# Modulation vectors from four stationary columns, and the first projections multiplied part by part

## The chip, the cores and the metric

One core of a Trainium2 chip runs the whole program. The metric is device time in microseconds (us) for one execution. The engines are called as in the profile: PE (TensorE, matmul), PEld (its weight loads), DVE (VectorE), ACT (ScalarE), POOL (GpSimd), SP (SyncE, which issues most DMAs).

## The reference, cut to what matters

The model is a block on 1024 tokens of width 1024 with a context of 256 tokens (an adaptive norm, a gated linear recurrence in two directions, a Fourier branch, 16 experts), and then a second mixer block. The change lies in its first steps only:

```
mx = silu(c)     @ w_ada + b_ada      # shift, scale, ... for the tokens
mc = silu(c_ctx) @ w_ada + b_ada      # the same for the context
pc = (rmsnorm(ctx, g) * (1 + csc1) + csh1) @ w_in    # gates, k, v of the context
px = (rmsnorm(x, g)   * (1 + sc1)  + sh1)  @ w_in    # all projections of the tokens
qk = silu(conv(px[q, k]));  gates -> log-sigmoid, running sums and maxima (scans)
```

Of `w_ada` only the first 2048 of 6144 columns (shift and scale of the first norm) are used in these steps.

## The kernel before, in words

Every large product is computed as three products of 32-bit operands that are split in a high and a low part: ACT copies the high part, DVE subtracts it from the operand to get the low part, and `mm3` (line 359) multiplies high by high, high by low and low by high into one PSUM bank. For a weight block of 128 x 1024, ACT and DVE each run one instruction for this (`_split`, line 234).

Each engine runs its instructions in the order in which the program emits them. All are issued through the wrapper at line 67, so that every row of the profile has the line L67; rows are told apart by their tiles: `w` split weights, `raw` weights as loaded, `silr` the split of silu(c), `ctx` and `x` the inputs, `hc` the modulated context (high and low), `hT` the modulated tokens, `tm` the modulated value before its split, `gt` the gate arrays, `qk` and `ko` convolution outputs, `pm` and `pa` the two groups of four PSUM banks, `wg` the gate weights.

The start (`start`, line 433) has these stages:

1. SP issues the eight 1 MB row blocks of `w_ada`, then the context (1 MB), the first gate weights come on ACT's queue; the tokens (4 MB) and two blocks of `w_in` follow after the first block of `w_ada` is used.
2. For each of the eight blocks: split in halves of 1024 columns, then `mm3` with a stationary operand of two columns (c and c_ctx), 12 matmuls of 512 columns in each block, 96 in all, into four banks.
3. Sums of squares and norm of the context, 16 transposes of it into four `pa` banks, copies of the two rows of results, 16 small transposes of them, and six small DVE instructions that form shift and scale.
4. Modulation of the context, in eight pieces k of 128 channels: ACT writes the high part, DVE the value, then DVE or POOL (in turn) subtracts for the low part.

Then `ctx_pass` (line 787) multiplies gates and values of the context, and `px_front` (line 866) the projections of the tokens, beginning with blocks 4 to 7 of 128 columns (the k half), each for tokens 0 to 511, tokens 512 to 1023, and the context. `tok` and `chan` call `pump`, which between matmul groups emits steps of work that waits in lanes: lane 0 holds `prep` (transposes and modulation of the tokens) and then the convolutions, lane 1 the gate work and the context's convolutions. A planner with its own cost model (`Plan`) decides by `until` and `calm` when a step is emitted; it is only a model, and the chip then runs what was emitted. The first token block is multiplied in the order tokens 0 to 511, context, tokens 512 to 1023, while `prep` goes on.

Of the kernel before, what the change touches and what calls it, by code (L numbers as in the profile page):

```python
# [9 lines left out]
FT = mybir.dt.float32  # L10
# [142 lines left out]
class Kern:  # L153
# [228 lines left out]
    def consts(self):  # L382
# [12 lines left out]
        self.silr = c([2, 16], "silr", FR)  # L395
        self.sx = c([8], "sx")
        self.shx = c([8], "shx")
# [5 lines left out]
        self.sctx, self.shctx, self.dnc = (self.state.t[:, i:i + 8] for i in (1976, 1984, 1992))  # L403
# [28 lines left out]

    def start(self):
# [7 lines left out]
        self.raw_max, self.limit, self.ahead, self.sub_max = 8, 8, 0, 0  # L441
        self.prefetch()
        nc.sync.dma_start(cs.t[:, :2048].rearrange("p (a d) -> p a d", a=2),
                          I["ctx"].rearrange("(a p) d -> p a d", p=128))
        xs = [self.slot(FT, "x") for _ in range(4)]
        xv = [xs[t // 2].t[:, (t % 2) * 1024:(t % 2) * 1024 + 1024] for t in range(8)]

        def load_x(p):
            nc.sync.dma_start(xs[p].t[:, :2048].rearrange("p (a d) -> p a d", a=2),
                              I["x"][p * 256:(p + 1) * 256].rearrange("(a p) d -> p a d", p=128))  # L450
        st = self.stat
        tm = self.slot(FT, "tm")

        def sumsq(tiles, a, both=False):
            for t, v in enumerate(tiles):
                o = st[:, a + t:a + t + 1]
                if both and t % 2:
                    nc.vector.scalar_tensor_tensor(self.hT[7].t[:, 0:1024], v, 1.0, v, op0=OP.mult, op1=OP.mult, accum_out=o)
                else:
                    nc.scalar.activation(tm.t[:, 0:1024], v, AF.Square, accum_out=o)  # L460

        def norm(tiles, a, engs=(nc.vector,)):
            n = len(tiles)
            self.inv_sqrt(st[:, 16 + a:16 + a + n], st[:, a:a + n], 1.0 / D, EPS)
            for t, v in enumerate(tiles):
                f = st[:, 16 + a + t:17 + a + t]
                e = engs[t % len(engs)]
                if e is nc.scalar:
                    e.activation(v, v, AF.Copy, scale=f)
                else:  # L470
                    e.tensor_scalar(v, v, f, None, op0=OP.mult)

        def modulate(items):
            for ps, hi, lo, tmp, s, sh, eng in items:
                nc.scalar.activation(hi, ps, AF.Identity, scale=s, bias=sh)
            for ps, hi, lo, tmp, s, sh, eng in items:
                nc.vector.tensor_scalar(tmp, ps, s, sh, op0=OP.mult, op1=OP.add)
            for ps, hi, lo, tmp, s, sh, eng in items:
                eng.tensor_sub(lo, tmp, hi.bitcast(FT))

        self.wg = self.load_wg()
        nc.scalar.dma_start(self.wr, I["w_r"])


        nc.scalar.activation(self.silr[:, 0], self.silc, AF.Copy)
        nc.vector.tensor_sub(self.silr[:, 1], self.silc, self.silr[:, 0].bitcast(FT))
        acc = [self.bank("pm") for _ in range(4)]
        row = self.slot(FT, "row")
        wsb = [self.slot(FR, "w") for _ in range(4)]
        for k in range(8):  # L490
# [12 lines left out]
            if k == 0:  # L503
                for p in range(4):
                    load_x(p)
                self.limit = 10
        self.raw_max, self.ahead, self.sub_max, self.limit = 2, 2, 3, self.limit2
        self.free(*wsb)
        self.hT = [self.slot(FR, "hT") for _ in range(8)]
        sumsq(cv, 8)  # L510
        norm(cv, 8)
        sumsq(xv[0:2], 0, True)
        pss = [self.bank("pa", (2, 2, 128)) for _ in range(4)]
        for kk in range(4):
            for i in range(2):
                for j in range(2):
                    nc.tensor.transpose(pss[kk][:, i, j], cv[j][:, (2 * kk + i) * 128:(2 * kk + i + 1) * 128], self.idn)
        for j in range(4):
            if j % 2:
                nc.scalar.activation(row.t[:2, j * 512:(j + 1) * 512], acc[j][:2], AF.Copy)  # L520
            else:
                nc.vector.tensor_copy(row.t[:2, j * 512:(j + 1) * 512], acc[j][:2])
        ps = self.bank("pm", (16, 2))
        for j in range(16):
            nc.tensor.transpose(ps[:, j], row.t[:2, j * 128:(j + 1) * 128], self.idn[:2, :2])
        self.free(row)
        ba = self.cols[:, C_BA:C_BA + 16]
        g1 = self.cols[:, C_G1:C_G1 + 8]
        for i, (s, sh) in ((1, (self.sctx, self.shctx)), (0, (self.sx, self.shx))):
            nc.vector.tensor_add(sh, ps[:, 0:8, i], ba[:, 0:8])  # L530
            nc.vector.scalar_tensor_tensor(s, ps[:, 8:16, i], 1.0, ba[:, 8:16], op0=OP.add, op1=OP.add)
            nc.vector.tensor_mul(s, s, g1)
        self.hc = [self.slot(FR, "hc") for _ in range(2)]
        self.hcv = []
        for kk in range(4):
            items = []
            for i in range(2):
                k = 2 * kk + i
                hi = self.hc[k // 4].t[:, (k % 4) * 512:(k % 4) * 512 + 256]
                lo = self.hc[k // 4].t[:, (k % 4) * 512 + 256:(k % 4) * 512 + 512]  # L540
                items.append((pss[kk][:, i].rearrange("p a b -> p (a b)"), hi, lo,
                              tm.t[:, 1024 + (k % 4) * 256:1280 + (k % 4) * 256],
                              self.sctx[:, k:k + 1], self.shctx[:, k:k + 1], nc.vector if i else nc.gpsimd))
                self.hcv.append((hi, lo))
            modulate(items)
        self.prefetch()
        sumsq(xv[2:4], 2, True)
        norm(xv[0:2], 0)
        norm(xv[2:4], 2, (nc.scalar, nc.vector))
        self.free(cs)  # L550
        self.hv = [(s.t[:, :1024], s.t[:, 1024:2048]) for s in self.hT]

        def prep():
            for hf in range(2):
                tiles = xv[hf * 4:hf * 4 + 4]
                for k in range(8):
                    if hf == 0 and k == 3:
                        sumsq(xv[4:8], 4, True)
                    if hf == 0 and k == 5:
                        norm(xv[4:8], 4, (nc.vector, nc.scalar))  # L560
                    yield from self.until(*(v[:, k * 128:(k + 1) * 128] for v in tiles))
                    ps = self.bank("pa")
                    for i in range(4):
                        nc.tensor.transpose(ps[:, i * 128:(i + 1) * 128], tiles[i][:, k * 128:(k + 1) * 128], self.idn)
                    c = slice(hf * 512, hf * 512 + 512)
                    modulate([(ps, self.hv[k][0][:, c], self.hv[k][1][:, c],
                               tm.t[:, 1024 + (k % 2) * 512:1536 + (k % 2) * 512],
                               self.sx[:, k:k + 1], self.shx[:, k:k + 1], nc.gpsimd if k % 2 else nc.vector)])
                    yield 1.3
                self.free(xs[2 * hf], xs[2 * hf + 1])  # L570
                self.prepared = False
            self.free(tm)
            self.prepared = True
        self.prepared = None
        self.prefetch()
        self.spawn(prep())
# [52 lines left out]
    def chan(self, w, hs, evac, cols=128, order=None):  # L629
# [3 lines left out]
        for ns in order or (range(len(hs)),):  # L633
            while order and ns[0] == 1 and not self.prepared:
                self._step(0)
# [1693 lines left out]
```

## Time and profile before

| | |
|---|---|
| device time, median of 3 runs (lowest to highest) | 1965.65 us (1965.07 to 1966.28) |
| the profiled execution's own time | 1969.11 us |
| its span, first to last instruction | 1967.3 us |
| PE busy | 1877.2 us, 95% of the span |
| DVE busy | 1422.5 us, 72% |
| ACT busy | 884.8 us, 45% |
| POOL busy | 216.5 us, 11% |
| granted PE clock, mean | 0.979 of full speed |
| the chain that ended last | PE 87%, DVE 7%, ACT 2%, DMA 2% |

A busy share says how long an engine was at work, not whether the end waited for it; the timeline and the idle times, with what ended them, say that. In a row of the timeline the first number is the start of a run of equal instructions, the second the time from the first's start to the last's end.

### The profile page before, as it was taken

How to read it: one execution, taken by the hardware profiler on the slowest of the kernel's cores; microseconds unless marked ns; L12 is line 12 of the kernel's file. 1: busy time of each engine (PE TensorE's matmuls, PEld its weight loads, DVE VectorE, ACT ScalarE, POOL GpSimd, SP SyncE). 2: the span in 40 equal slices, each digit the busy share in tenths (PEclk: the TensorE clock that was granted, in tenths of full speed). 3: DMA queues.
4: the chain of work that ended last, by engine and by line, in shares of the span. 5: the costliest groups of instructions: out<-in, count | busy, mean ns of one | idle time of the engine just before them, and what ended most of it. 6: DMA issues, size and time to landing. Idle time of an engine off the chain costs nothing.

```text
span 1967.3 us, 23992 instructions
## 1 busy us (share of the span) xinstructions
PE 1877.2 (95%) x9258; PEld 1516.7 (77%) x9258; DVE 1422.5 (72%) x2111; ACT 884.8 (45%) x1256; POOL 216.5 (11%) x187
## 2 busy tenths in 40 slices
PE   6899999999999999859999999999989999999997
PEld 3687888888877787647888888888868977678786
DVE  7797675555653645779999999999983877563554
ACT  6623432222232233227777777777864223342300
POOL 1300000000000006442100101001030000000011
PEclk9999999999999999969999999999989999999999
DMA  8100125533323533468999999999951110011312
GB/s 352 65 26 22 46 88 213 183 130 128 118 86 131 180 118 129 158 259 322 368 386 380 373 388 410 395 396 387 393 186 43 33 42 23 28 44 43 128 64 75
DMA packets 64541, 361.03 MB, mean 184 GB/s; under 512 B 9742, under 2 KB 10775, under 8 KB 30380
## 3 DMA queue, kind: packets, MB, share of 16 engines
q1 hardware_dynamic: 50508, 318.17, 41.7%
q0 software_dynamic: 9824, 35.42, 5.8%
q10 hardware_dynamic: 4096, 5.91, 0.9%
q8 instruction: 73, 1.20, 0.2%
q14 instruction: 40, 0.33, 0.1%
HBM read 329.96 MB, written 29.52 MB: 183 GB/s over the span
## 4 chain that ended last, share of the span: by engine, by line
PE 87%; DVE 7%; ACT 2%; DMA 2%; issue 1%; POOL 1%; POOLq 0%; ACTq 0%; DVEq 0%; SPq 0%
PE pm L67 76%; PE pa L67 11%; DVE tk L67 2%; DMA bd<-gd 1%; DVE gt L67 1%; DVE tx L67 1%; POOL w L67 1%; DVE w L67 0%; DMA wgr<-in_w_g 0%; DVE tm L67 0%; ACT gt L67 0%; DMA b<-yd 0%; DVE mw L67 0%; ACT x L67 0%; ACT w L67 0%
## 5 line engine op out<-in xcount | busy, mean ns | idle before, releaser
L67 DVE TENSOR_TENSOR w<-raw,w 128x1024 fp32r<-128x1024 f32 (+1 forms) x496 | 587.0, 1226 | 83.1 <-ACT w L67 79.9
L67 ACT ACTIVATE w<-raw 128x1024 fp32r<-128x1024 f32 (+1 forms) x504 | 510.3, 1052 | 106.1 <-PE pm L67 99.4
L67 PE MATMUL pm<-w,xT 128*128 128x512 f32 x2304 | 553.0, 397 | 4.7 <-POOL w L67 3.4
L67 PEld LDWEIGHTS pm<-w,xT 128*128 128x128 f32 x2304 | 429.4, 189 | 101.5 <-POOL w L67 5.6
L67 PE MATMUL pm<-hT,w 128*128 128x512 f32 x1536 | 384.2, 402 | 0.0
L67 PEld LDWEIGHTS pm<-hT,w 128*128 128x128 f32 x1536 | 284.7, 191 | 60.7 <-issue 1.7
L67 PE MATMUL pm<-x,w 128*128 128x512 f32 x1152 | 281.7, 400 | 0.0
L67 PEld LDWEIGHTS pm<-x,w 128*128 128x128 f32 x1152 | 214.0, 188 | 54.5 <-issue 8.4
L67 PE MATMUL pm<-w,hh 128*128 128x512 f32 x480 | 111.4, 393 | 1.0 <-DVE w L67 1.0
L67 PEld LDWEIGHTS pm<-w,hh 128*128 128x128 f32 x480 | 90.1, 188 | 22.1 <-DVE w L67 1.3
L67 PE MATMUL pm<-w,mg 128*128 128x512 f32 x384 | 97.5, 402 | 0.0
L67 POOL DMA_INDIRECT x1d<-xs,idx x16 | 44.3, 2768 | 385.5 <-DVE xs L67 378.0
L67 PEld LDWEIGHTS pm<-w,mg 128*128 128x128 f32 x384 | 69.4, 188 | 16.2 <-issue 1.5
L67 DVE SCALAR_TENSOR_TENSOR qk<-raw,cols,qk 128x945 f32<-128x945 f32 (+2 forms) x64 | 78.0, 1219 | 1.3
L67 DVE SCALAR_TENSOR_TENSOR dg<-da,cols,dg 128x1023 f32<-128x1023 f32 (+29 forms) x60 | 76.0, 1267 | 1.6
L67 POOL TENSOR_SCALAR sm<-sm 128x1 f32<-128x1 f32 x16 | 11.2, 703 | 363.3 <-DVE sm L67 362.6
L67 ACT ACTIVATE xT<-pa 128x512 fp32r<-128x512 f32 x64 | 37.6, 590 | 30.1 <-PE pa L67 30.0
L67 DVE TENSOR_TENSOR xT<-pa,xT 128x512 fp32r<-128x512 f32 x64 | 43.6, 682 | 7.2 <-ACT xT L67 7.2
L67 ACT ACTIVATE b<-pm 128x512 f32<-128x512 f32 x32 | 19.1, 598 | 66.0 <-PE pm L67 63.1
L67 PEld LDWEIGHTS pm<-w,hT 128*128 128x128 f32 x384 | 46.0, 189 | 2.2 <-ACT w L67 0.9
L67 PE MATMUL pm<-w,hT 128*128 128x256 f32 x384 | 46.8, 283 | 0.2 <-DVE w L67 0.2
L67 PE MATMUL pm<-om,w 128*128 128x512 f32 x192 | 45.2, 395 | 1.7 <-ACT om L67 1.0
(366 smaller groups left out, 2081.3 us busy)
## 6 DMA issues: line engine op xcount, KB each, us to landing
raw<-in_w_gate SPq DMA_DIRECT2D x64, 1024.0 KB, 8.3
raw<-in_w_down SPq DMA_DIRECT2D x64, 1024.0 KB, 7.1
raw<-in_w_up SPq DMA_DIRECT2D x63, 1024.0 KB, 12.4
raw<-in_w_in SPq DMA_DIRECT2D x34, 1024.0 KB, 5.2
raw<-in_w_ada_rest SPq DMA_DIRECT2D x16, 1024.0 KB, 6.6
raw<-in_w_out SPq DMA_DIRECT2D x9, 1024.0 KB, 4.8
raw<-in_w_ada SPq DMA_DIRECT2D x8, 1024.0 KB, 12.2
b<-yd SPq DMA_DIRECT2D x16, 512.0 KB, 3.5
```

The source lines that it names most:

```text
L67: return f(*a, **kw)
```

## The change

The diff has five parts. (a) The stationary operand holds four columns, high and low parts of c and c_ctx; each block of `w_ada` takes 8 matmuls in place of 12, and the four result rows are added after the small transposes. (b) The context is loaded first, its squares are taken before the first block is split, its norm and transposes stand inside the loop over the blocks; the gate weights are prepared after block 4 of 8. (c) Modulation no longer uses POOL: ACT writes the high part, and for odd k also the value; DVE writes the value for even k, and all low parts. (d) In `ctx_pass` each modulated piece of the context is multiplied for the gates and for the first half of the values as soon as it is there; the second half of the values, the tokens' squares and the norm of tokens 0 to 511 follow. (e) `front_blocks` replaces `prep` and the special order of the first block: for each k it transposes and modulates, multiplies the context for blocks 4 and 5, and the piece before for both blocks. It calls no `pump`; gates and convolutions start behind it, with lane 0 at rate 1.4 in place of 3 and then 1.

```diff
+    def modulate(self, ps, hi, lo, tmp, s, sh, on_act):
...
+        nc.scalar.activation(hi, ps, AF.Identity, scale=s, bias=sh)
+        if on_act:
+            nc.scalar.activation(tmp, ps, AF.Identity, scale=s, bias=sh)
+        else:
+            nc.vector.tensor_scalar(tmp, ps, s, sh, op0=OP.mult, op1=OP.add)
+        nc.vector.tensor_sub(lo, tmp, hi.bitcast(FT))
...
+        nc.sync.dma_start(cs.t[:, :2048].rearrange("p (a d) -> p a d", a=2),
+                          I["ctx"].rearrange("(a p) d -> p a d", p=128))
...
+        self.raw_max, self.limit, self.ahead, self.sub_max = 10, 10, 0, 4
+        while self.u_issued < 10:
+            self._issue()
...
+        nc.scalar.activation(self.silr[:, :, 0:2], pairs, AF.Copy)
+        nc.vector.tensor_sub(self.silr[:, :, 2:4], pairs, self.silr[:, :, 0:2].bitcast(FT))
+        self.sumsq(cv[0:1], 8, [tm.t[:, 0:1024]])
+        self.sumsq(cv[1:2], 9, [tm.t[:, 0:1024]])
...
-            for j0 in range(0, 4, 1 if k == 7 else 2):
-                js = range(j0, j0 + (1 if k == 7 else 2))
+            n = 1 if k in (0, 7) else 2
+            for j0 in range(0, 4, n):
+                js = range(j0, j0 + n)
...
-                    self.mm3(acc[j][:2], [self.silr[:, i, k::8] for i in range(2)], [x.t[:, c] for x in ws],
-                             k == 0, k == 7)
+                    for i in range(2):
+                        nc.tensor.matmul(acc[j][:4], self.silr[:, k], ws[i].t[:, c],
+                                         start=k == 0 and i == 0, stop=k == 7 and i == 1)
...
+                self.norm(cv, 8)
+                self.limit = 12
+            if k == 1:
+                for kk in range(4):
+                    for i in range(2):
+                        for j in range(2):
+                            nc.tensor.transpose(pss[kk][:, i, j], cv[j][:, (2 * kk + i) * 128:(2 * kk + i + 1) * 128],
+                                                self.idn)
+            if k == 4:
+                self.wg = self.load_wg()
...
+        nc.vector.tensor_reduce(modr, ps.rearrange("p j (a i) -> p i j a", a=2), axis=AX.X, op=OP.add)
...
-        self.chan(wg, hs, g_evac, cols=100)
-        self.rate[0] = 2.0
...
+        for k in range(8):
+            self.modulate(self.pss[k // 2][:, k % 2].rearrange("p a b -> p (a b)"), *hcv[k],
...
+            if k in (1, 4):
+                wv.append(self.get())
+            self.mm3(gps[:100, :256], (wg[1][:, k, :100], wg[2][:, k, :100]), hcv[k], k == 0, k == 7)
+            js = {0: (), 1: (0, 1)}.get(k, (k,))
+            for j in js:
+                w = wv[j // 4]
+                for t in range(2):
+                    self.mm3(v0[t][:, :256], tuple(a[:, t * 128:(t + 1) * 128] for a in hcv[j]),
+                             (w[1][:, j % 4], w[2][:, j % 4]), j == 0, j == 7)
...
+        g_evac([gps])
+        self._step(1)
+        for t in range(2):
+            v_evac(0, t, v0[t][:, :256])
...
+        wv = [self.get(), self.get()]
...
+        self.sumsq(self.xv[0:4], 0, [s.t[:, 0:1024] for s in self.hT[6:8]])
+        for t in range(2):
...
+            v_evac(1, t, ps[:, :256])
...
+        self.norm(self.xv[0:4], 0)
...
+        ws = [self.get(), self.get()]
...
+            def x(k):
+                for j, w in enumerate(ws):
+                    self.mm3(out[j][n], (w[1][:, k], w[2][:, k]), tuple(a[:, c] for a in self.hv[k]), k == 0, k == 7)
+            for k in range(8):
+                ps = self.bank("pa")
+                for i in range(4):
+                    nc.tensor.transpose(ps[:, i * 128:(i + 1) * 128], tiles[i][:, k * 128:(k + 1) * 128], self.idn)
+                self.modulate(ps, *(a[:, c] for a in self.hv[k]), tm.t[:, 1024 + (k % 2) * 512:1536 + (k % 2) * 512],
+                              self.sx[:, k:k + 1], self.shx[:, k:k + 1], k % 2)
+                if n == 0:
+                    for j, w in enumerate(ws):
+                        self.mm3(out[j][2][:, :256], (w[1][:, k], w[2][:, k]), self.hcv[k], k == 0, k == 7)
+                    if k == 2:
+                        self.sumsq(xv[4:8], 4, [tm.t[:, 0:1024], self.hT[7].t[:, 0:1024]])
+                    if k == 4:
+                        self.norm(xv[4:8], 4)
+                if k:
+                    x(k - 1)
+            x(7)
+            self.free(self.xs[2 * n], self.xs[2 * n + 1])
+        half(0)
+        half(1)
...
+        self.raw_max, self.ahead, self.sub_max, self.limit = 2, 2, 3, self.limit2
+        self.prefetch()
```

## Rows read from the trace of the kernel before

**Rows 1.** The page's first part: busy us (share of the span) and instructions.

```profile
PE 1877.2 (95%) x9258; PEld 1516.7 (77%) x9258; DVE 1422.5 (72%) x2111; ACT 884.8 (45%) x1256; POOL 216.5 (11%) x187
```

**Rows 2.** Stretches: from:to and length, engines' busy us, PEclk, DMA share, GB/s; loading.

```profile
0.00:5.00 5.00, 0.00 (x0) 0.00 (x0) 0.56 (x6) 1.50 (x2) 0.19 (x4) 1.00 0.61 212
5.00:10.00 5.00, 0.00 (x0) 0.00 (x0) 1.75 (x1) 0.00 (x0) 0.00 (x0) 1.00 1.03 423
```

**Rows 3.** Timeline up to 40 us: start, length, engine, operation, count, idle before.

```profile
4.99 1.76 DVE L67 MEMSET wg<- 128x2048 f32 x1 [0.38 <-issue]
13.33 23.09 PE L67 MATMUL pm<-w,silr 128*2 128x512 f32 x95 [0.67 <-DVE w L67]
29.24 3.63 DVE L67 TENSOR_TENSOR w<-raw,w 128x1024 fp32r<-128x1024 f32 x5 [0.17 <-ACT w L67]
...
32.62 1.06 ACT L67 ACTIVATE tm<-ctx 128x1024 f32<-128x1024 f32 x1
...
34.87 1.42 DVE L67 TENSOR_SCALAR ctx<-ctx,stat 128x1024 f32<-128x1024 f32 x2 [2.00 <-POOL stat L67]
...
37.35 1.27 DVE L67 COPY row<-pm 2x512 f32<-2x512 f32 x2
...
39.90 3.75 ACT L67 ACTIVATE hc<-pa,state 128x256 fp32r<-128x256 f32 x8 [2.85 <-DVE state L67]
```

**Rows 4.** Timeline from 40 to 61 us: context products, modulation of the first token pieces.

```profile
40.95 1.00 DVE L67 TENSOR_SCALAR tm<-pa,state 128x256 f32<-128x256 f32 x2 [0.80 <-ACT hc L67]
...
47.14 2.35 DVE L67 TENSOR_TENSOR w<-raw,w 128x1024 fp32r<-128x1024 f32 x2
...
48.18 6.64 PE L67 MATMUL pm<-w,hc 128*128 128x256 f32 x48
...
53.61 0.94 ACT L67 ACTIVATE gt<-pm,bgc 36x256 f32<-36x256 f32 x2
...
58.21 1.03 PE L67 MATMUL pa<-kc,x 128*128 128x128 f32 x8
...
59.53 0.78 ACT L67 ACTIVATE hT<-pa,shx,sx 128x512 fp32r<-128x512 f32 x1
59.67 0.81 DVE L67 TENSOR_SCALAR tm<-pa,sx,shx 128x512 f32<-128x512 f32 x1 [0.15 <-ACT hT L67]
...
60.51 0.69 DVE L67 TENSOR_TENSOR hT<-tm,hT 128x512 fp32r<-128x512 f32 x1
```

**Rows 5.** Timeline from 70 to 186 us: norm, token blocks, the transposes of the gate arrays.

```profile
70.11 2.19 ACT L67 ACTIVATE x<-x,stat 128x1024 f32<-128x1024 f32 x2 [4.62 <-POOL stat L67]
...
109.69 1.55 PE L67 MATMUL pm<-hT,w 128*128 128x512 f32 x6
...
138.08 7.06 PE L67 MATMUL pm<-hT,wg 128*100 128x512 f32 x30
...
185.86 1.68 PE L67 MATMUL pa<-kc,gt 36*128 36x36 f32 x16 [2.09 <-DVE gt L67]
```

**Rows 6.** Stretches around PE's idle times, columns as in rows 2.

```profile
43.00:49.00 6.00, 5.66 (x23) 4.63 (x22) 5.90 (x11) 3.58 (x6) 4.01 (x5) 0.50 0.18 72
54.00:57.00 3.00, 1.40 (x9) 0.99 (x9) 1.22 (x1) 2.96 (x6) 0.00 (x0) 1.00 0.00 0
66.00:70.00 4.00, 0.66 (x4) 0.42 (x4) 2.89 (x5) 0.00 (x0) 2.72 (x3) 1.00 0.00 0
70.00:77.00 7.00, 5.74 (x19) 4.23 (x20) 5.25 (x7) 6.74 (x9) 1.84 (x3) 0.51 0.00 0
```

**Rows 7.** Stretches behind the first two token blocks, columns as in rows 2.

```profile
100.00:160.00 60.00, 60.00 (x310) 49.73 (x309) 56.53 (x73) 13.88 (x21) 1.24 (x4) 1.00 0.08 22
160.00:180.00 20.00, 20.00 (x92) 16.09 (x91) 11.57 (x14) 10.75 (x12) 0.04 (x1) 1.00 0.00 0
```

**Rows 8.** One stretch, instructions of one tile only: `gt`, then `qk` (without POOL).

```profile
87.50:109.70 22.20, 0.31 (x2) 0.20 (x2) 5.97 (x16) 2.09 (x5) 1.33 (x2) 1.00 0.17 49
87.50:109.70 22.20, 0.00 (x0) 0.00 (x0) 7.91 (x7) 0.00 (x0) 1.00 0.17 49
```

More of the change, by code (lines that the diff above doesn't have):

```diff
@@ L430, in consts, with sumsq, norm @@
         self.yd = self.dp.tile([8, 128, 1024], FT, name="yd")
+    def sumsq(self, tiles, a, junk):
+        nc = self.nc
+        for t, v in enumerate(tiles):
+            o = self.stat[:, a + t:a + t + 1]
+            if t % 2:
+                nc.vector.scalar_tensor_tensor(junk[1], v, 1.0, v, op0=OP.mult, op1=OP.mult, accum_out=o)
+            else:
+                nc.scalar.activation(junk[0], v, AF.Square, accum_out=o)
+    def norm(self, tiles, a):
+        nc = self.nc
+        st, n = self.stat, len(tiles)
+        self.inv_sqrt(st[:, 16 + a:16 + a + n], st[:, a:a + n], 1.0 / D, EPS)
+        for t, v in enumerate(tiles):
+            f = st[:, 16 + a + t:17 + a + t]
+            if t % 2:
+                nc.scalar.activation(v, v, AF.Copy, scale=f)
+            else:
+                nc.vector.tensor_scalar(v, v, f, None, op0=OP.mult)
+    def modulate(self, ps, hi, lo, tmp, s, sh, on_act):
+        nc = self.nc
+        nc.scalar.activation(hi, ps, AF.Identity, scale=s, bias=sh)
+        if on_act:
+            nc.scalar.activation(tmp, ps, AF.Identity, scale=s, bias=sh)
+        else:
+            nc.vector.tensor_scalar(tmp, ps, s, sh, op0=OP.mult, op1=OP.add)
+        nc.vector.tensor_sub(lo, tmp, hi.bitcast(FT))
     def start(self):
@@ L451, in start @@
[L451 to L471, printed above, removed]
@@ L489, in start @@
         wsb = [self.slot(FR, "w") for _ in range(4)]
+        pss = [self.bank("pa", (2, 2, 128)) for _ in range(4)]
         for k in range(8):
@@ L506, in start @@
[L506 to L517, printed above, removed]
+                self.norm(cv, 8)
@@ L521, in start @@
             else:
-                nc.vector.tensor_copy(row.t[:2, j * 512:(j + 1) * 512], acc[j][:2])
-        ps = self.bank("pm", (16, 2))
+                nc.vector.tensor_copy(row.t[:4, j * 512:(j + 1) * 512], acc[j][:4])
+        self.free(*wsb)
+        ps = self.bank("pm", (16, 4))
         for j in range(16):
[L525 to L532, printed above, removed]
-        self.hc = [self.slot(FR, "hc") for _ in range(2)]
[L534 to L573, printed above, removed]
@@ new lines, in start @@
+            nc.tensor.transpose(ps[:, j], row.t[:4, j * 128:(j + 1) * 128], self.idn[:4, :4])
+        self.free(row, cs)
+        nc.scalar.dma_start(self.wr, I["w_r"])
+        modr = tm.t[:, 2048:2080].rearrange("p (a b) -> p a b", a=2)
+        nc.vector.tensor_reduce(modr, ps.rearrange("p j (a i) -> p i j a", a=2), axis=AX.X, op=OP.add)
+        two = lambda a: self.cols[:, a:a + 8][:, None, :].to_broadcast([128, 2, 8])
+        scale = self.mod1[:, 1]
+        nc.vector.scalar_tensor_tensor(scale, modr[:, :, 8:16], 1.0, two(C_BA + 8), op0=OP.add, op1=OP.add)
@@ L574, in start @@
+        nc.vector.tensor_mul(scale, scale, two(C_G1))
+        nc.vector.tensor_add(self.mod1[:, 0], modr[:, :, 0:8], two(C_BA))
+        self.hc = [self.slot(FR, "hc") for _ in range(2)]
+        self.hcv = [(self.hc[k // 4].t[:, (k % 4) * 512:(k % 4) * 512 + 256],
+                     self.hc[k // 4].t[:, (k % 4) * 512 + 256:(k % 4) * 512 + 512]) for k in range(8)]
+        self.pss = pss
         self.prepared = None
-        self.prefetch()
-        self.spawn(prep())
     def add_px(self):
@@ L626, in add_px, with chan @@
             self.add(self.I["w_out_2"][i // 2], "k")
-    def chan(self, w, hs, evac, cols=128, order=None):
+    def chan(self, w, hs, evac, cols=128):
         hi, lo = w[1], w[2]
         pss = [self.bank("pm" if n < 2 else "pa") for n in range(len(hs))]
-        for ns in order or (range(len(hs)),):
-            while order and ns[0] == 1 and not self.prepared:
-                self._step(0)
-            if order and ns[0] == 1:
-                self.rate[0] = 1.0
-            for k in range(8):
-                for n in ns:
-                    h = hs[n][k]
-                    N = h[0].shape[1]
-                    self.mm3(pss[n][:cols, :N], (hi[:, k, :cols], lo[:, k, :cols]), h, k == 0, k == 7)
-                if k < 7:
-                    self.pump(0.65 * len(ns))
+        for k in range(8):
+            for n in range(len(hs)):
+                h = hs[n][k]
+                N = h[0].shape[1]
+                self.mm3(pss[n][:cols, :N], (hi[:, k, :cols], lo[:, k, :cols]), h, k == 0, k == 7)
+            if k < 7:
+                self.pump(0.65 * len(hs))
         evac(pss)
@@ L816, in g_evac @@
                                   lambda v: [(v["wa"], self.gcolc)], after), 1)
-        self.chan(wg, hs, g_evac, cols=100)
-        self.rate[0] = 2.0
+        tm, hcv = self.tm, self.hcv
+        gps, v0 = self.bank("pm"), [self.bank("pm") for _ in range(2)]
+        wv = []
+        for k in range(8):
+            self.modulate(self.pss[k // 2][:, k % 2].rearrange("p a b -> p (a b)"), *hcv[k],
+                          tm.t[:, 1024 + (k % 4) * 256:1280 + (k % 4) * 256],
+                          self.sctx[:, k:k + 1], self.shctx[:, k:k + 1], k % 2)
+            if k in (1, 4):
[7 more added lines that the diff above has]
+                             (w[1][:, j % 4], w[2][:, j % 4]), j == 0, j == 7)
+        for w in wv:
+            self.done(w)
+        v_evac = lambda u, t, ps: nc.scalar.activation(
+            vav[:, 2 * u:2 * u + 2, t, 0:128], ps.rearrange("p (h v) -> p h v", h=2), AF.Copy)
+        g_evac([gps])
+        self._step(1)
+        for t in range(2):
+            v_evac(0, t, v0[t][:, :256])
         def kgen(h):
@@ L879, in g_evac @@
                                              (v["wa"], self.gcol[:, 2])], after), 1)
[L880 to L882 removed]
+        self.rate = [1.4, 1.0, 1.0, 1.0]
         hx = self.hx
@@ L886, in px_front @@
         for i, blk0 in enumerate((4, 6, 0, 2)):
+            first = self.front_blocks() if i == 0 else None
             raw = self.slot(FT, "raw2")
@@ L903, in evac @@
                     self.spawn(self.conv(r, o, blk, 16, lambda: self.free(raw) if j else None))
-                self.chan(w, hx + [self.hcv] if i < 2 else hx, evac, order=None if i or j else ((0,), (2,), (1,)))
+                if first:
+                    evac(first[j])
+                    continue
+                w = self.get()
+                self.chan(w, hx + [self.hcv] if i < 2 else hx, evac)
                 self.done(w)
@@ L916, in px_front, with front_blocks, half @@
         self.mlstm_values()
+    def front_blocks(self):
+        nc = self.nc
+        ws = [self.get(), self.get()]
+        tm, xv = self.tm, self.xv
+        out = [[None] * 3 for _ in ws]
+        def half(n):
+            c = slice(n * 512, n * 512 + 512)
+            tiles = xv[4 * n:4 * n + 4]
+            for j in range(2):
+                out[j][n] = self.bank("pm")
+                if n == 0:
+                    out[j][2] = self.bank("pa")
+            def x(k):
+                for j, w in enumerate(ws):
+                    self.mm3(out[j][n], (w[1][:, k], w[2][:, k]), tuple(a[:, c] for a in self.hv[k]), k == 0, k == 7)
+            for k in range(8):
+                ps = self.bank("pa")
[3 more added lines that the diff above has]
+                              self.sx[:, k:k + 1], self.shx[:, k:k + 1], k % 2)
+                if n == 0:
+                    for j, w in enumerate(ws):
[10 more added lines that the diff above has]
+        half(1)
+        for w in ws:
+            self.done(w)
+        self.free(tm)
+        self.prepared = True
+        self.raw_max, self.ahead, self.sub_max, self.limit = 2, 2, 3, self.limit2
+        self.prefetch()
+        return out
     def fourier_in(self):
```

58 lines of the change are left out of this document (21 added, 37 removed).

## The prediction

> **What bounds the kernel now.** I read the page's busy shares first, then stretches, then the timeline of the first 190 us with the idle times and what ended them. PE is busy for 95% of the span [rows 1], and from 100 us on it has hardly a gap: 60.0 of 60 us between 100 and 160 [rows 7]. So a change ahead of that is worth what it brings the first full-rate stretch of PE forward, and nothing else; all later work should move with it. The marker I use is the first matmul of token block 6, behind blocks 4 and 5 and their context parts: 109.69 us [rows 5]. [...] From 13.3 to 36.4 us PE runs 95 matmuls without a gap [rows 3]: this stage waits for PE, with the loads at the full rate of 423 GB/s [rows 2]. [...]
>
> **The change, step by step.**
>
> *Stage of w_ada, to the first modulation.* PE falls from 96 to 64 matmuls, 15 us of work, so PE no longer sets the end. Loading: 1.06 MB are in at 5.0 us, then 2.5 us for each MB [rows 2]; the constants (0.36 MB by their widths) and the context, now first, are in at 5.9, the first block at 8.4, the last at 25.9. DVE is later than both. It begins at 9.05, after ACT's two squares (1.06 each) and a first high part. Then: 8 quarters of 512 columns at 0.60 (of five in 3.63, one takes 1.2) = 4.8; 12 halves at 1.17 (two in 2.35 [rows 4]) = 14.0; one of the two norm multiplies, 0.7; the memset of the gate weights, 1.76, which before lay in free time at 5 us, with some 0.5 of small subtracts; two waits for ACT, 2.0 together (ACT's own norm multiply ahead of block 1; ACT's gate-weight copies wait for that memset, and block 5's split is queued behind them) [rows 3]. Sum 23.8, end 32.85. Two row copies, 1.27, end at 34.1; from there to the first modulation before took 39.90 - 38.62 = 1.28 [rows 3], with one more dependent small instruction 1.5: 35.7 in place of 39.90. **Gain 4.2 us.** If the memset and the waits were hidden it would be 8.5, if ACT waited longer 2.
>
> *Context and values.* Before, DVE's read of a bank waited for ACT's read of it (0.80 idle at 40.95, 0.15 at 59.67 [rows 4]), and pieces k and k+1 of the context share a bank. So a pair costs ACT 0.47, DVE 0.5, ACT 0.47 twice, with hand-overs 2.1 us, and with two splits on ACT all eight pieces last to 46.4. The first values need the low part of their weights: 35.7 + 2.1 + 1.05 (ACT) + 1.17 (DVE) = 40.0. Then 66 matmuls of 256 columns at 0.125 (48 in 6.64, of which the first ran at the low clock [rows 4]) end at 48.2. ACT evacuates gates (0.94 [rows 4]) and values (0.75), and only then splits the second pair of weights, whose first low part is ready at 51.4: **PE idle 3.2 us.** 48 matmuls, 6.0, end at 57.5. In ACT's queue the norm of the tokens (two in 2.19 [rows 5]) stands behind the evacuation of these, the splits of blocks 4 and 5 behind the norm: 57.9, 60.1, 62.2, low part 63.4, first context piece 63.8. **PE idle some 5 us again.**
>
> *Token blocks.* For one k PE has 4 transposes (0.11 each by eight in 1.03, 0.44), six context matmuls 0.75, six of 512 columns at 0.23 (30 in 7.06) 1.38 [rows 4, 5]: 2.57 us. The way from the transposes to a low part is 0.17 + 0.78 (ACT) + 0.81 (DVE) + 0.69 (DVE) [rows 4] + hand-overs 0.1 = 2.53, just covered for tokens 0 to 511: 7 x 2.57 + 1.78 + 0.3 for the squares and norm of the other half = 20.1. For the other half there are no context matmuls to cover it. PE waits in x(k-1), the next transposes queued behind; two steps then take 2.53 + 1.82, so 2.18 each: 4.35 + 7 x 2.18 = 19.6. End 103.5; block 6 then waits about 0.7 for ACT to empty two `pm` banks: 104.2. **Against 109.69 a gain of 5.5.**
>
> [...] DVE started on a bank when ACT left it [rows 4]. [...]
>
> *Clock.* PE stood idle for most of 66 to 70 us, and 70 to 77 us were granted 0.51; after the shorter gap in 54 to 57 us it stayed at 1.00 [rows 6]. My gaps are 35 to 40, 48.2 to 51.4 and 58 to 63 us. I let the first and the third cost a fall, 1.3 us each (a fall of 6 to 7 us that lies partly over waiting), and the second none, since it is nearest to that of 54 to 57. Bounds: 0 for all three, 3 each. **Loss 2.6, net gain 2.9 us.**
>
> *POOL's subtracts* go to DVE (8 at 0.69 and 4 at about 0.35, 6.9 us), half of DVE's value passes to ACT (8.0 us off DVE): priced above, nothing more; neither is full in 64 to 104 us.
>
> *Vector work put behind.* `front_blocks` emits no waiting work. The context's gate chain (DVE 6.0 us) and the first block's convolution (7.9), done by 109.7 before [rows 8], with the context's convolution about 1.3, come after it: 15 us. DVE has 3.5 idle in 100 to 160 and 8.4 in 160 to 180 [rows 7], and the convolutions are not needed for long. I price this at 0, and keep -1 (the planner's order also changes for the better) and +12 as ends.
>
> *The loads* are no bound: two more `w_in` blocks are asked for inside the loop, behind the tokens on SP's queue, and in at about 46 us, needed at 60.
>
> The sum is made against the profiled execution: 1969.11 - 2.9 = 1966.2. That execution is 3.5 us above the median of the runs, a difference that the change doesn't touch, so for the median 1965.65 - 2.9 = 1962.75, rounded **1963 us**.
>
> **Rivals.**
> - *The overlap is better than my queues allow.* PE's clock never falls, the memset hides, and the serial waits at 48 and 58 us shrink: gain 5.5 plus up to 4, 1956 to 1960, say 1958. For it: PE has only some 53 us of work between 35.7 and 104. Against it: both gaps follow from the order in ACT's queue.
> - *The front comes out even.* All three gaps bring a clock fall at 2 each, or ACT's evacuations wait for the context's gate work in its queue: 5.5 - 6 = 0, 1966. For it: two falls in the trace of before in the same part [rows 6].
> - *Slower: the work put behind lands on PE.* In-order PE already waits 2.09 us at 185.86 for the tokens' gate arrays, whose scans DVE runs last [rows 5]. If the 15 us are emitted ahead of those scans, DVE's 11.9 us of idle time up to 180 don't hold them, and PE waits 3 us or more, at most the whole 15, and then works at the low clock for some 3 more. With 8 us in all less 2.9: 1971. It decides when more than some 6 us (the 2.9 gained and a fall) remain. For it: DVE is 94% busy in 100 to 160 us. Against it: convolutions give way in the planner when DVE is ahead of PE by more than 3 us.
>
> **How the numbers follow.** My forecast (1960.5 to 1965.5 as its own range) gets 0.45, the better overlap 0.25, the even case 0.10, the slower one 0.20. 0.2% is 3.9 us, so faster means below 1961.7: 0.16 of the forecast's share and the first rival's 0.25 give 0.41. Within 0.2%: 0.29 of the forecast, 0.10 of the even case and 0.02 of the slower one, 0.41. Slower: 0.18. The range must reach into both sides: low 1955.5, where all falls are absent and something more is hidden; high 1972, a little beyond the slower case's middle.
>
> **What would show it.** 64 matmuls with four columns, the last of them at about 33.3 us, DVE nearly without gaps from 9 us; first `hc` row at 35.7 (above 38: the stage is wrong). PE idle near 48 to 51 us and 58 to 63 us, ended by ACT or DVE rows of `w` and `x`; granted clock of 0.5 behind the first and the third. In the second half of `front_blocks` PE waits behind DVE's `hT` in periods of 2.2 us. Block 6 at about 106.8 us. The transposes of the tokens' gate arrays should come within some 3 us of 185.9; if PE waits there for more than 5 us, the slower rival holds. The forecast is wrong if block 6 moves by less than 1 or more than 6 us, or if that shift isn't found in the end of the span.

## The result: slower by 1.1%, and the loss lies behind the front

The changed kernel took 1989.85 us (median; 1989.41 to 1990.74), the kernel before 1965.97 us in the same comparison: ratio 1.0111, 95% interval 1.0093 to 1.0129 (the quotient of the two medians is 1.0121). I had said 1963 us. The profiled execution took 1989.62 us, its span is 1987.7 us against 1967.3.

The page of the changed kernel, its busy shares and the shares of the chain by engine:

```profile
PE 1876.5 (94%) x9226; PEld 1516.6 (76%) x9226; DVE 1416.4 (71%) x2109; ACT 895.3 (45%) x1274; POOL 201.8 (10%) x173
PE 82%; DVE 11%; ACT 3%; issue 2%; DMA 1%; POOL 1%; POOLq 0%; DVEq 0%; SPq 0%; ACTq 0%
```

Against [rows 1] PE has 0.7 us less to do and DVE 6.1 us less. PE's idle time grew from 90.1 to 111.2 us, and on the chain that ended last PE has 82% in place of 87%, DVE 11% in place of 7%. So 20 us were lost to waiting, not to work.

First the front, which the forecast was about. Timeline of the changed kernel up to the first matmul of block 6, answering to [rows 3 to 5] (start, length, engine, operation, idle before):

```profile
6.87 1.06 ACT L67 ACTIVATE tm<-ctx 128x1024 f32<-128x1024 f32 x1 [2.53 <-DMA ctx<-in_ctx]
...
36.93 0.56 ACT L67 ACTIVATE hc<-pa,state 128x256 fp32r<-128x256 f32 x1 [1.26 <-DVE vac L67]
...
53.11 0.38 PE L67 MATMUL pm<-w,hc 128*128 128x256 f32 x1 [1.96 <-ACT w L67]
54.37 7.36 PE L67 MATMUL pm<-w,hc 128*128 128x256 f32 x47 [0.88 <-DVE w L67]
...
63.24 0.44 PE L67 MATMUL pa<-kc,x 128*128 128x128 f32 x2 [1.40 <-ACT x L67]
64.28 0.33 PE L67 MATMUL pa<-kc,x 128*128 128x128 f32 x1 [0.60 <-ACT x L67]
65.22 0.50 PE L67 MATMUL pa<-hc,w 128*128 128x256 f32 x2 [0.61 <-ACT w L67]
66.48 1.72 PE L67 MATMUL pa<-hc,w 128*128 128x256 f32 x4 [0.76 <-DVE w L67]
...
96.96 1.41 PE L67 MATMUL pm<-hT,w 128*128 128x512 f32 x5 [0.39 <-DVE hT L67]
...
101.25 1.43 PE L67 MATMUL pm<-hT,w 128*128 128x512 f32 x5 [0.38 <-DVE hT L67]
...
108.85 1.43 PE L67 MATMUL pm<-hT,w 128*128 128x512 f32 x5 [0.24 <-ACT raw L67]
```

The reader sees the first modulation at 36.93 (39.90 before), the two forecast gaps of PE, the second half in periods of 4.29 us for two steps (96.96 to 101.25), and block 6 at 108.85 in place of 109.69: 0.84 us gained. That gain is smaller than the scatter between executions: with this same front block 6 came between 108.41 and 110.40 us in seven traces (this one and those of experiments 1, 2, 3, 5, 9 with 1, and 12), with the front of before at 109.69 and, in experiment 12, at 111.20. Up to here nothing is lost.

The loss lies behind. The first Fourier matmul (`pm<-w,ee`), first before, then in the changed kernel:

```profile
253.12 1.61 PE L67 MATMUL pm<-w,ee 128*128 128x258 f32 x12
277.05 1.70 PE L67 MATMUL pm<-w,ee 128*128 128x258 f32 x12
```

It begins 23.9 us late, so 24.8 us were lost between it and block 6. Later stages give 3.5 of them back. PE's waits between 108 and 285 us in the changed kernel (us in total, times, longest):

```profile
PE pa L67 <- DVE gt L67: 12.4, 1, 12.4
PE pm L67 <- DVE w L67: 3.3, 1, 3.3
PE pa L67 <- ACT gt L67: 3.1, 1, 3.1
PE pa L67 <- ACT ft L67: 1.4, 2, 0.9
PE pm L67 <- ACT w L67: 1.2, 1, 1.2
```

With 0.7 us of smaller ones these are 22.1 us; the kernel before has 2.1 there, the wait of [rows 5]. So 20 of the 24.8 are waits. The rest is PE at work for longer on nearly the same matmuls, 4.9 us between the two marks, at a lower granted clock, 0.92 in place of 0.98 (columns as in rows 2; first before, then the changed kernel):

```profile
109.69:253.12 143.43, 141.34 (x676) 115.15 (x675) 113.26 (x162) 51.27 (x74) 3.27 (x7) 0.98 0.11 37
108.85:277.05 168.20, 146.27 (x678) 118.39 (x679) 127.77 (x180) 57.61 (x80) 6.20 (x11) 0.92 0.08 24
```

What PE waits for are the tokens' gate arrays (`gt`). All of DVE's scans on them in the changed kernel, with the time of one in ns (shortest, median, longest), and first and last start:

```profile
L67 DVE TENSOR_TENSOR_SCAN gt<-gt x2: 673/676/679, 158.0 to 158.7; 32x256 f32<-32x256 f32 x1, 4x256 f32<-4x256 f32 x1
L67 DVE TENSOR_TENSOR_SCAN gt<-gt,stat x2: 739/740/740, 159.4 to 160.2; 32x256 f32<-32x256 f32 x1, 4x256 f32<-4x256 f32 x1
L67 DVE TENSOR_TENSOR_SCAN gt<-gt,gt x2: 2272/2276/2280, 251.3 to 253.6; 32x1024 f32<-32x1024 f32 x1, 4x1024 f32<-4x1024 f32 x1
L67 DVE TENSOR_TENSOR_SCAN gt<-gt,state x2: 2339/2340/2340, 255.9 to 258.3; 32x1024 f32<-32x1024 f32 x1, 4x1024 f32<-4x1024 f32 x1
```

The context's (256 wide) ran at 90.9 us before and run at 158.0; the tokens' (1024 wide) ran at 174.6 and run at 251.3. On DVE before:

```profile
90.87 1.37 DVE L67 TENSOR_TENSOR_SCAN gt<-gt 32x256 f32<-32x256 f32 x2
...
97.78 0.76 DVE L67 TENSOR_SCALAR qk<-raw,cols 128x1024 f32<-128x1024 f32 x1 [1.23 <-ACT raw L67]
...
174.55 4.57 DVE L67 TENSOR_TENSOR_SCAN gt<-gt,gt 32x1024 f32<-32x1024 f32 x2
```

In the changed kernel DVE wasn't idle ahead of the tokens' scans:

```profile
222.24 1.21 DVE L67 SCALAR_TENSOR_TENSOR gt<-gt 36x1024 f32<-36x1024 f32 x1
226.96 1.22 DVE L67 SCALAR_TENSOR_TENSOR gt<-gt,gt 36x1024 f32<-36x1024 f32 x1 [3.50 <-ACT gt L67]
...
235.99 4.99 DVE L67 SCALAR_TENSOR_TENSOR qk<-raw,cols,qk 128x945 f32<-128x945 f32 x4
...
247.73 3.69 DVE L67 SCALAR_TENSOR_TENSOR qk<-raw,cols,qk 128x945 f32<-128x945 f32 x3
251.34 4.57 DVE L67 TENSOR_TENSOR_SCAN gt<-gt,gt 32x1024 f32<-32x1024 f32 x2
```

Between the gates' last step before the scans (it ends at 228.2) and the scans stand, apart from three splits of weights, taps of convolutions (`qk`); none of PE's waits above is for them. **Theory A, starvation:** a gate generator gives way (`calm`) while DVE's planned time is over 3 us ahead of PE's. The token convolutions are a queue of their own, are served first, and each tap fills DVE up to that very lead. By this theory the gates pass only when the convolutions are through, and everything behind them in their queue (context keys, values, tokens' gates, folds) is late with them. Before, the context's scans ran ahead of the first step of any convolution (97.78).

### The profile page after: what moved, and what is told of

Its sections match the earlier page's. It is cut to its first block, busy times and chain, and to the rows that moved or that the text cites. A ratio compares the mean times of both kernels' runs of the same rounds, so it can differ in the third digit from the quotient of the medians.

```text
span 1987.7 us, 23930 instructions
## 1 busy us (share of the span) xinstructions
PE 1876.5 (94%) x9226; PEld 1516.6 (76%) x9226; DVE 1416.4 (71%) x2109; ACT 895.3 (45%) x1274; POOL 201.8 (10%) x173
## 4 chain that ended last, share of the span: by engine, by line
PE 82%; DVE 11%; ACT 3%; issue 2%; DMA 1%; POOL 1%; POOLq 0%; DVEq 0%; SPq 0%; ACTq 0%
PE pm L67 72%; PE pa L67 10%; DVE qk L67 3%; DVE tk L67 2%; DVE w L67 1%; DVE gt L67 1%; ACT w L67 1%; POOL w L67 0%; DVE tx L67 0%; DMA raw<-in_w_ada 0%; DVE at L67 0%; DVE dg L67 0%; DMA bd<-gd 0%; ACT gt L67 0%; DVE mw L67 0%
## 5 line engine op out<-in xcount | busy, mean ns | idle before, releaser
L67 PEld LDWEIGHTS pm<-w,hh 128*128 128x128 f32 x480 | 90.1, 188 | 22.5 <-DVE w L67 1.3
```

The costliest lines, as they stand in the source:

```text
L67: return f(*a, **kw)
```

## Experiments

Each ratio is against the kernel before in the same comparison (its median varied from 1968 to 1970 us between chips). In the kernel before, `mm3` stands at line 354, `ctx_pass` at 790 and `px_front` at 868.

**1. The context's gates don't give way.**

```
-        yield from self.calm()
+        if T != CTX:
+            yield from self.calm()
```

> The changed kernel, but the context's gates don't wait for VectorE's planned lead to fall below 3 us (calm) ahead of their scans. Theory A (the gate work of the context is starved: its generator stands at that wait until the token convolutions are all in, and everything that comes after it in the same queue is late): the scan that ran at 158 us runs at 115 to 122 us, the matmul that waited 12.4 us for the tokens' gates at 262.7 us waits less than 3 us, and the time is 1965 us, give or take 4. Rival B (the vector work that the change moved behind block 6 is simply too much, 15 us of it, whatever its order): the wait on PE stays or moves, 1980 us or more.

Ratio 1.0056 [1.0037, 1.0076]. The scan runs at 116.8 us and the wait for the gates is gone, as A said; half of the loss is not, and with 1980.68 us and a wait that moved B's mark is met too. PE now waits for pieces of weights:

```profile
PE pm L67 <- ACT w L67: 11.4, 2, 6.2
PE pm L67 <- DVE w L67: 1.9, 2, 1.5
```

The same kernel's timeline shows why they are late, though ScalarE has time (4.3 of 20 us busy in 180 to 200):

```profile
177.03 1.06 ACT L67 ACTIVATE gt<-gt 36x1024 f32<-36x1024 f32 x1
178.11 1.08 ACT L67 ACTIVATE u<-pm 128x512 f32<-128x512 f32 x2
179.08 1.06 ACT L67 ACTIVATE w<-raw 128x1024 fp32r<-128x1024 f32 x1
...
180.19 1.22 PE L67 MATMUL pm<-hT,w 128*128 128x512 f32 x2 [5.16 <-ACT w L67]
...
194.87 1.06 ACT L67 ACTIVATE qk<-qk 128x1024 f32<-128x1024 f32 x1 [13.43 <-DVE qk L67]
...
199.48 1.06 ACT L67 ACTIVATE gt<-gt 36x1024 f32<-36x1024 f32 x1 [2.25 <-DVE gt L67]
...
201.40 1.99 ACT L67 ACTIVATE w<-raw 128x1024 fp32r<-128x1024 f32 x2
...
202.50 1.22 PE L67 MATMUL pm<-hT,w 128*128 128x512 f32 x2 [6.23 <-ACT w L67]
```

The weight copy isn't made ahead, but when its block is due, behind the gates' chain: PE is through with the block before at 196.3, and ahead of the copy (201.40) stand in ScalarE's queue a gate activation, which DVE's scans release at 199.48, and the evacuation of that block. The 13.43 us for which ScalarE waits before, while PE still works, are room that a copy made ahead would have had. A is right on the scan and on the wait for the gates, not on the time; B is not refuted yet.

**2. Rate 1.0 for the convolutions** (`self.rate = [1.0, 1.0, 1.0, 1.0]`).

> The changed kernel with the token convolutions' queue run at rate 1.0 in place of 1.4 at the start. Theory A (starvation at calm): the convolutions still fill VectorE's lead and the context's scan still comes last, 1980 to 1990 us. Rival C (the rate of 1.4 on the convolutions' queue is what lets them crowd the gates out): the scan comes by 125 us and the time falls to 1966 us, give or take 4.

1.0047 [1.0032, 1.0063], 1979.43 us. A missed: the scan doesn't come last but at 124.8 us, as C said, so less push does end the starvation, and the rate of 1.4 is one of its conditions. C missed on the time, which is no better than in 1 within the intervals. The waits are the same ones for weights (9.8 and 1.3 us).

**3. The gates' queue is served first** (`pump` steps lane 1 ahead of lane 0).

> The changed kernel with the gates' queue served ahead of the convolutions' queue at every step of the planner's pump, all through the kernel. Theory A: the gates find VectorE's lead below 3 us now and then, the scan comes by 125 us, and the time is 1966 us, give or take 6 (the order changes elsewhere too). Rival B (amount of vector work, not order): 1980 us or more.

1.0071 [1.0047, 1.0095]. The scan comes at 117.4, the tokens' scans at 175.1 as before the change, and still PE waits 10.9 us for `w` on ACT. A's time failed here too (1983.55 us, B's side): three cures of the starvation leave the same second wait.

**4. Starvation put into the kernel before.** Its front stays; the context's scans are held back.

```
+        while T == CTX and not self.eager and not self.held:
+            yield 0.25
```

(`held` is set once the tokens' gate columns are multiplied.)

> The kernel before, unchanged in its front, but the context's gate scans are held until the tokens' gate columns have been multiplied (the scan moves from 91 us to about 150 us or later). Theory A: the loss of the changed kernel appears without the change, 1980 to 1990 us, with a wait of PE for the tokens' gates near 240 us. Rival B (it takes the moved vector work) or rival D (something else of the change, its clock or its loads): within 3 us of 1966 us.

1.0062 [1.0042, 1.0082], with no part of the change in it. Held to 147.0 us in place of 158.0 it loses some 12 us, less than expected, at weights (6.0 and 1.6 us) and at the folds (`ft`, 3.2), and the wait for the tokens' gates that I expected near 240 us isn't there. Late gates of the context alone are a loss, about half of the whole, but here too most of the waiting is for weights.

**5. Less vector work.** Experiment 1, and block 4's convolution computes only its centre tap (eight of nine taps are left out).

> The changed kernel without the context gates' wait for VectorE (as in the first experiment), and the token convolution of block 4 computes only its centre tap: its eight side taps, 9.6 us of VectorE work, are left out. What is left of the loss there (PE waits of 11.4 us for weight copies on ScalarE and 1.9 us on VectorE between 175 and 205 us) comes, by theory B2, from the amount of vector work that now lies behind block 6: with 9.6 us of it gone, the waits fall below 4 us and the time is at most 1.001 of the kernel before. By rival E (the order on ScalarE's queue alone: a weight copy stands behind the activation that ends a convolution, whatever the amount) the waits stay above 8 us and the ratio above 1.003.

1.0013 [1.0003, 1.0023], but ACT's `w` still ends 9.0 us of waiting. Neither had it: 8 of the 11 us left in 1 go with the work, the wait for a copy in its wrong place stays. That turned me from how much work there is to why no copy is made ahead.

**6 to 8. Filling the second half, a lag of two, an earlier front.** In 6, key blocks are evacuated after the first half, the gates no longer wait for the end of the modulation, and their queue gets turns in the second half:

```
+                if n:
+                    self.pump(1.3)
```

> The changed kernel with its second half of the first two blocks (tokens 512 to 1023, where VectorE is busy half of the time) filled: the context's key blocks are evacuated after the first half, and each step of the second half gives the gates' queue a turn (context's gates, then two context convolutions). Theories A and B2 (the lost time is vector work put behind block 6, starved and then crowding): the scan that ran at 158 us runs at 92 to 102 us, PE waits less than 4 us between 160 and 285 us, and the time is 0.997 to 1.003 of the kernel before. Rival F (vector work in the second half lengthens its latency-bound steps, 4.29 us for two, by as much as it saves later): block 6 comes 5 us or more later than 108.9 us and the ratio stays above 1.004.

In 7, products two steps behind the transposes there (`x(k - 1 - n)`).

> The kernel of the filled second half, with the products of that half two steps behind the transposes in place of one. If the period of 4.29 us for two steps is the latency from transpose over ScalarE and VectorE to the product, as I forecast, it falls to the matmuls' own 3.6 to 3.7 us and block 6 comes 2 to 3 us earlier than with the fill alone; the time falls by 1 to 3 us. If it is VectorE's or ScalarE's load, the period stays above 4.1 us and nothing moves.

In 8, splits, squares and norm moved ahead of the second values, context products of two k ahead of the first transposes.

> The kernel of the filled second half and the lag of two, with three steps of the front moved ahead: the splits of the second value weights come with the last context block, the tokens' squares and norm come before the second values are multiplied, and the splits of the first blocks' weights come ahead of those values; the context's key products of two k run ahead of the first token transpose. The PE waits at 51 to 54 us (2.8) and 61.6 to 66.5 us (about 4.5) go, the first token transposes come by 58 us in place of 63.2, block 6 at 99 to 103 us; the time is 4 to 7 us below the kernel with the lag alone, so below the kernel before. Rival G (the earlier front collides with the loads, or the clock falls by as much): block 6 comes less than 2 us earlier.

1.0077 [1.0061, 1.0094], 1.0078 [1.0061, 1.0095] and 1.0060 [1.0044, 1.0077]. F's marks are met in 6: the scan runs at 97.1 us, but the pumped work stands in ACT's queue ahead of the modulation and block 6 comes at 113.92; 9.7 us of waits for weights stay, so A and B2 missed on the waits and the time. In 7 block 6 comes at some 112.4 (12 matmuls behind 109.44, of 18 in 4.45 us), 1.5 us earlier in place of 2 to 3, and the time doesn't fall: two steps take 3.65 us, as expected, only where no gate work stands between them (97.69 to 101.34). In 8 it comes at 105.6 (12 of 18 in 4.43 behind 102.69), later than the 99 to 103 expected, and the time falls by about 3.5 us, not below the kernel before: the front's gain is there (with the same front block 6 came at 107.9 in 10 and 108.6 in 9 with 8), 11.6 us of waits for weights take it.

**9. One buffer fewer in reserve.** A piece is split ahead only if more buffers are free than the reserve `spare`, 2 in this stage. The last convolutions hold an input buffer (`raw2`) when the tokens' gates take three: **theory H**, the late work costs a buffer, and with it the lead of the weights.

```
     def fourier_in(self):
-        self.spare = 2
+        self.spare = 1
```

> The first experiment's kernel (context gates without the wait for VectorE), with one buffer fewer kept in reserve while the four Fourier input blocks are multiplied (spare 1 in place of 2), so that a weight piece can be split ahead although the last token convolutions still hold their input buffer when the tokens' gates take three. Theory H (buffers: the late convolutions hold one buffer too many, no weight piece is split ahead, its copy is put on ScalarE's queue behind the gates' chain and PE waits 13.3 us for it between 175 and 205 us): these waits fall below 3 us and the time to at most 1.001 of the kernel before. Rival B2 (VectorE has too much to do whatever is split ahead): the waits stay at 8 us or more, or move to the gates' values, and the ratio stays at 1.004 or more.

With 1: 0.9994 [0.9982, 1.0005]. The waits for weights are gone; PE's largest between 108 and 285 us are

```profile
PE pa L67 <- ACT gt L67: 2.0, 1, 2.0
PE pa L67 <- DVE gt L67: 0.9, 1, 0.9
```

> The kernel with the earlier front and the filled second half, and the same one buffer of reserve fewer. Theory H: of its 11.7 us of waits for weight pieces between 174 and 201 us at most 3 are left, and the time is 0.996 to 0.999 of the kernel before. Rival B2: the waits stay or move to the gates' values, 1.003 or more.

With 8: 0.9960 [0.9946, 0.9974], from 1.0060, and no wait for weights is left. H meets both expectations. B2 meets neither: the same vector work stands behind block 6 with and without the edit.

**10. The buffer by another way.** In 8's kernel the tokens' gates take buffers only when the convolutions are through.

> The kernel with the earlier front and the filled second half, reserve as it was, but the tokens' gates take their three buffers only when the token convolutions are through (so the weight pieces find a free buffer by another way). Theory H: waits for weight pieces near 175 to 200 us go, but the gates' values come later, so part of it comes back as a wait for them or at the folds after: 0.997 to 1.003 of the kernel before. Rival B2: 1.004 or more with the same waits.

0.9995 [0.9984, 1.0005]; 3.8 us of waits for weights remain, at 213 us. The time and the waits near 175 to 200 us are as H says; the wait for the gates' values or at the folds that should have come in their place isn't there.

**11. The repaired kernel**: earlier front, lag of two, 1 and the smaller reserve, no fill.

> The kernel with the earlier front and one buffer of reserve fewer, its second half not filled (context gates and convolutions come behind it, the gates without the wait for VectorE). Theory H with the front's gain: block 6 comes at 100 to 103 us in place of 109.7 in the kernel before, no wait above 3 us after it, and the time is 0.995 to 0.998 of the kernel before. Rival B2 (the vector work behind block 6 decides, so filling matters and the reserve does not): slower than the filled kernel with the same reserve, 1.002 or more.

0.9943 [0.9926, 0.9960]: 1961.31 us (1957.25 to 1961.97), faster than both kernels, somewhat beyond the best expected. Block 6 comes at some 100.3 us (18 matmuls behind 95.99, of 24 in 5.81 us), and PE's only wait from 108 to 285 us is

```profile
PE pa L67 <- DVE gt L67: 0.4, 1, 0.4
```

Steps of its second half, without fill, run at PE's pace, 1.83 us for one in place of 2.15:

```profile
91.98 0.60 PE L67 MATMUL pa<-kc,x 128*128 128x128 f32 x4
...
93.81 0.60 PE L67 MATMUL pa<-kc,x 128*128 128x128 f32 x4
...
95.63 0.60 PE L67 MATMUL pa<-kc,x 128*128 128x128 f32 x4
```

DVE has the same 1416.3 us to do, the context's gates and convolutions still lie behind block 6, and nothing is lost by it: the amount of that work by itself was not the cause (B2 falls here too), though less of it helps (5).

**12. Controls: the smaller reserve alone**, in the kernel before and in the changed one.

> The kernel before with nothing but one buffer fewer in reserve (spare 1 in place of 2) while the Fourier input blocks are multiplied. Theory H (the buffer matters only where late convolutions take the place of a piece split ahead; in the kernel before the pieces are ahead already and PE has only the 2.1 us wait near 186 us): 0.998 to 1.001. Rival K (the smaller reserve is a gain of its own, which the experiments with it took for a repair): 0.994 to 0.997.

0.9995 [0.9985, 1.0004]: no gain of its own.

> The changed kernel with nothing but the same one buffer fewer in reserve; the context's gates are starved as they were. Theory A with H (two causes that add, starvation and the buffer): the scan stays at about 158 us and the waits for the tokens' gates near 262 us (12.4 and 3.1 us) stay, the two waits for weights near 212 us (1.2 and 3.3 us) go, the ratio is 1.006 to 1.010. Rival L (the buffer alone carries the whole loss, and starvation follows from it): at most 1.002.

1.0136 [1.0114, 1.0158], worse than both said. The scan stays at 157.6 us and the waits for the gates stay (10.5 and 3.1 us), as A with H said, but the waits for weights don't go: they are 9.0 us in place of 4.5. The buffer alone cures nothing, and on the weights H missed here. Its tokens' scans show the starvation at its plainest, on DVE:

```profile
227.64 2.27 DVE L67 TENSOR_TENSOR_SCAN gt<-gt,gt 32x1024 f32<-32x1024 f32 x1
229.84 0.72 DVE L67 TENSOR_SCALAR qk<-raw,cols 128x1024 f32<-128x1024 f32 x1
230.59 10.04 DVE L67 SCALAR_TENSOR_TENSOR qk<-raw,cols,qk 128x945 f32<-128x945 f32 x8
...
247.27 10.04 DVE L67 SCALAR_TENSOR_TENSOR qk<-raw,cols,qk 128x945 f32<-128x945 f32 x8
257.34 2.28 DVE L67 TENSOR_TENSOR_SCAN gt<-gt,gt 4x1024 f32<-4x1024 f32 x1
```

Two scans of one chain, 29.7 us apart, with two whole convolutions between them. So the causes are two: starvation is shown by 1, 4 and this run, the buffer by 9 against 1 and against 8. They don't simply add: the reserve helped where the gates were on time and not where they were late. That the late convolution's `raw2` is the very buffer that is missing follows from the code and fits 9 and 10; no run frees that buffer alone. How much of the 24.8 us each has is therefore not one number; I leave it at 1.0111 with both, 1.0056 without the first, 0.9994 without either.

## Why the prediction was wrong, by its steps

- *Stage of w_ada.* Forecast 35.7, measured 36.93: the context was in at 6.87, not 5.9; the serial DVE sum behind it held to 0.3 us. Gain 3.0 in place of 4.2.
- *PE's gaps.* Forecast 3.2 and 5, measured 2.8 (1.96 and 0.88) and 3.4 (1.40, 0.60, 0.61, 0.76). Right in place and cause; experiment 8, by moving the splits ahead in ACT's queue, removed the first and left 2.5 us of the second.
- *Token steps.* 4.29 us for two against 4.35 forecast. That the chain of one step sets it, not an engine's load, is shown by 11, where a lag of two brings PE's own pace, 1.83 us for one. DVE's read of a bank began 0.03 us after ACT's read of it had ended (99.66 us, behind 98.85 and 0.78); what this wait costs by itself was not tried.
- *Clock.* I charged a fall behind the first and the third gap. All three had one (the granted clock is the third number from the end):

```profile
38.00:46.00 8.00, 6.64 (x29) 5.93 (x30) 6.09 (x12) 6.20 (x11) 0.00 (x0) 0.57 1.03 415
...
50.00:55.00 5.00, 2.17 (x16) 1.76 (x15) 1.91 (x2) 4.48 (x8) 0.00 (x0) 1.00 0.00 0
55.00:62.00 7.00, 6.84 (x45) 6.60 (x44) 4.24 (x7) 1.81 (x5) 1.21 (x2) 0.76 0.00 0
...
66.00:72.00 6.00, 5.39 (x19) 4.71 (x20) 3.67 (x5) 2.23 (x4) 0.00 (x0) 0.50 0.00 0
```

  The fall behind the second gap, which I put at none, is not in every trace: 47 matmuls of the second values took 7.36 us here, 8.38 in experiment 2 and 5.84 in 6, at granted clocks of 0.83, 0.69 and 1.00 in 50 to 60 us. With it and the late context, less the shorter second wait, block 6 comes at 108.85, not 106.8: of 2.9 us forecast 0.84 arrived. By my own sign (a shift of less than 1 us) the forecast of the front failed too, on its size; its places held.
- *"Vector work put behind ... I price this at 0."* This is the step that failed, by 24.8 us, twice its own bound of 12. I compared an amount (15 us) with idle time (11.9 us). What the work does to the planner's queues I left out: it puts gates that give way beside convolutions that refill, at a rate of 1.4 that the change brings, and the late work keeps buffers that the weight pieces need. The runs show it in the context's scans (158.0 us in place of 90.9), in PE's waits (22.1 us in place of 2.1 between 108 and 285 us), and in experiment 9, which has the same work behind block 6 and no loss (0.9994).
- *The slower rival* had kind and mark right, PE waiting for the tokens' gate arrays behind DVE's scans, more than 5 us. Its price of 8 was three times too small and its place (185.9, the wait came at 262.7) 77 us too early, because it let 15 us of work be late and not a whole queue. My argument against it, that convolutions give way when DVE is more than 3 us ahead, is the mechanism itself: gates give way by the same rule, and the convolutions keep DVE at that mark.

## What to carry to other kernels

Work that gives way to a full engine hardly runs beside work that keeps the engine full to the same mark (here the scans came 67 us late, and 34 us late when the other work was pushed at a lower rate); before moving such work, ask in which queue it will stand and what else feeds that engine then, not only how many microseconds there are. Work that ends later also holds its buffers later, and the first to miss one may be a prefetch on another engine: look at whether the weights' copies still run a block ahead. A small change of order is judged at the far end of its queue; here 0.8 us gained at 109 us, no more than scatter, stood against 24.8 lost by 277.

## What the runs showed of the hardware

In the changed kernel a scan over 1024 columns took VectorE 2.27 to 2.34 us, with 32 rows or with 4, where an elementwise operation on 36x1024 took 1.21; four of them were 9.3 us in one chain. From 256 to 1024 columns the scan grew by 1.60 us (0.68 to 2.28), the elementwise operation by 0.80 (0.41 to 1.21), half as much. And in experiment 1 PE waited 6.2 us for weight copies of 1.0 us each on ScalarE, which stood in its queue behind a gate activation that VectorE's scans released only at 199.48, 3.2 us after PE had run out of work. ScalarE was busy for 4.3 of the 20 us before 200: an engine that was mostly idle was the one that PE waited for, because the copies ran behind that activation.
